# Two blocks on one core: block compression with the weights moving in four column groups, gate activations in table order, the decay moved, operand splits shared

## The chip, the cores and the metric

The program runs on one core of one Trainium2 chip. The metric is the device time of one execution in microseconds (us). The engines are TensorE (PE in the profile, its weight loads PEld), VectorE (DVE), ScalarE (ACT), GpSimd (POOL) and SyncE (SP), which here only issues the loads of weights. TensorE's granted clock has two levels, 2.4 GHz (1.00 in the profile) and 1.2 GHz (0.50).

## The reference

The first block is two layers of attention, pooling, convolution and FFN over 256 tokens and 256 context tokens. The second is one hybrid layer over the 256 tokens of the result, and the change is in it. Cut to what it touches:

```python
# NSA branch: 15 blocks of 32 tokens, stride 16, of k and v, for 2 kv heads
def compress(t, w1, w2):
    tb = t[:, blk_idx] + cmp_pos[None, None, :, None, :]
    tb = tb.transpose(0, 1, 3, 2, 4).reshape(B, n_cmp, G, CMP_BLOCK * dh)   # 2048 features
    return jax.nn.silu(tb @ w1) @ w2                                        # 128 hidden, 64 out
k_c = rms_norm_2(compress(k_cmp, wk1, wk2), kn_g)
v_c = compress(v_cmp, wv1, wv2)
...
# LRU branch
r = jax.nn.sigmoid(...); i_g = jax.nn.sigmoid(...)
log_a = -LRU_C * r * jax.nn.softplus(-lam)
a = jnp.exp(log_a)
b = jnp.sqrt(-jnp.expm1(2.0 * log_a)) * (i_g * xc)
...
# fox branch
c = jnp.cumsum(jax.nn.log_sigmoid(f_logit), axis=1)   # added to the scores
# the branches and their gates
y_a * silu(ga), y_b * silu(gb), y_c * silu(gc), y_d * silu(gd)   # y_d = gelu(ud) * mix(layer_norm(gelu(vd)))
```

## The kernel before

**Products.** Activations lie transposed, 128 features by 256 tokens a tile. Almost every product of weights is made of three matmuls in the type fp32r (`mm3`, lines 354 to 356: hi times hi, hi times lo, lo times hi). `weights()` (lines 339 to 348) brings 128x1024 weights in one 512 KB load issued by SP (line 336), ACT casts them to `whi` (line 344) and DVE subtracts for `wlo` (line 345). The pools hold 4 raw tiles, 3 `whi` and 3 `wlo`, so a cast waits until the products of the third chunk before are done. `split` (lines 350, 351) does the same to an activation. `evac` copies from PSUM in turn on ACT (line 678) and on DVE (line 680).

**Order.** The program is written in the order of its loops, and a list scheduler with a model of the durations sets the order of each engine's instructions from the dependences. `tc.issue_after(i)` adds the edge that what is issued inside comes after `i`.

**Compression** (lines 1137 to 1175). DVE adds the position (line 1137) and gives `tbs[p]`, 128 features by 16 chunks of 32 columns. For k and then for v, 16 fp32 matmuls (line 1146) have a 128x128 chunk of `w1` as the stationary operand and 32 columns of `tbs` as the moving one, and add into 128 hidden by 32 columns; an fp32 matmul is two records in the trace, so there are 64. Silu on ACT (line 1149) gives `hT`. From that of k follow a matmul with `w2` (line 1152), ACT's square (line 1155), DVE and POOL for the norm, DVE `kc` (line 1160) and a transpose (line 1162); from that of v, lines 1166 to 1175.

**Decay and forget gates** (lines 1217 to 1254). `log_sigmoid` is ACT's Abs and Exp and then a series of 20 small DVE operations. It is used for 16 columns of `lsig` (the fox cumulative sum, two matmuls) and for 4 columns of `lam2`, from which `cneg` and `cpos` are scaled.

**NSA heads, gates, fox heads** (lines 1298 to 1580). `jobs` holds 20 projections for branch b and d, and later 8 for `ga` and `gc`; `more(n)` takes n of them between heads. Eight NSA heads (scores, `probs`, `weighted`) run, then `batch` issues the 12 gate activations (Sigmoid, Gelu, Silu) on ACT (line 1458) after the last Exp of the last NSA head. Eight fox heads follow. `probs` puts min and mask on DVE (line 1390), Exp on ACT (line 1393), the scaling on DVE (line 1398). `weighted` has three transposes (line 1421), a copy `aT`, and two matmuls (lines 1424, 1425). After fox head 0, `lru_gates()` issues four times Tanh and Exp in turns (lines 1349, 1350); ACT loads a table whenever a function of another table comes.

**After the fox heads**, `late_gates` and the merge by the mixing gates (lines 1592 and on) follow.

Of the kernel before, what the change touches and what calls it, by code (L numbers as in the profile page):

```python
# [12 lines left out]
F32 = mybir.dt.float32  # L13
# [212 lines left out]
def _constants():  # L226
# [31 lines left out]
    parts["rep"] = rep  # L258
    off, flat = 0, []
# [17 lines left out]
def tile_two_blocks(ctx: ExitStack, tc: tile.TileContext, w: bass.AP, blk: bass.AP, cols: bass.AP,  # L277
# [4 lines left out]
    P = {"nscr": NSCR}  # L282
# [612 lines left out]
    rows = modulation_by_rows()  # L895
    for l in range(DEPTH):
# [91 lines left out]
        for t, (f0, f1) in enumerate(THIRDS):  # L988
# [3 lines left out]
            for f in range(f0, f1):  # L992
# [19 lines left out]
                rows_step(0)  # L1012
            final = t == 2
# [203 lines left out]
    def log_sigmoid(dst, x, n, y_out=None):  # L1217

        e, z, z2, s = (P["wk"].tile([128, 16], F32, name="ls", bufs=5)[:, :n] for _ in range(4))
        act.activation(e, x, AF.Abs)  # L1220
        act.activation(e, e, AF.Exp, scale=-1.0)
        dve.tensor_scalar(z, e, 2.0, None, op0=ALU.add)
        dve.reciprocal(z, z)
        dve.tensor_tensor(z, z, e, op=ALU.mult)
        dve.tensor_tensor(z2, z, z, op=ALU.mult)
        dve.tensor_scalar(s, z2, 2.0 / 17, 2.0 / 15, op0=ALU.mult, op1=ALU.add)
        for i in (13, 11, 9, 7, 5, 3, 1):
            dve.tensor_tensor(s, s, z2, op=ALU.mult)
            dve.tensor_scalar(s, s, 2.0 / i, None, op0=ALU.add)
        dve.tensor_tensor(s, s, z, op=ALU.mult)  # L1230
        dve.scalar_tensor_tensor(dst, x, 0.0, s, op0=ALU.min, op1=ALU.subtract)

    fox_side("ka", "kna", 1.0)
    fox_side("qa", "qna", -0.125)

    ls = P["wk"].tile([128, 2, 8], F32, name="lsig")
    for i, tt in enumerate(TT):
        dve.tensor_tensor(ls[:, i], small[tt][:, 280:288], R("bf"), op=ALU.add)
    log_sigmoid(ls.rearrange("p a b -> p (a b)"), ls.rearrange("p a b -> p (a b)"), 16)
    cneg = P["wk"].tile([128, 4], F32, name="cneg")  # L1240
    cpos = P["wk"].tile([128, 4], F32, name="cpos")
    log_sigmoid(cneg, C("lam2"), 4)
    dve.tensor_scalar(cneg, cneg, 8.0, None, op0=ALU.mult)
    dve.tensor_scalar(cpos, cneg, -1.0, None, op0=ALU.mult)
    for i, tt in enumerate(TT):
        ps = bank("aux")
        for j in range(i + 1):
            pe.matmul(ps[:, :8], K("tri") if j == i else ones, ls[:, j], start=(j == 0), stop=(j == i))
        zq, zk = qk66["qa", tt], qk66["ka", tt]
        dve.tensor_scalar(zq[:, :, 64], ps[:, :8], -1.0, None, op0=ALU.mult)  # L1250
        dve.tensor_copy(zk[:, :, 65], ps[:, :8])
        pool.memset(zq[:, :, 65:66], 1.0)
        pool.memset(zk[:, :, 64:65], 1.0)
# [14 lines left out]
    for i, tt in enumerate(TT):  # L1268
# [24 lines left out]
        evac(pcT[:, i * 128:i * 128 + 128], pt[:, :128])  # L1293

# [88 lines left out]
    last_exp = [None]  # L1383

    def probs(items, gates):
# [3 lines left out]
        for i, (ps, mask, e) in enumerate(items):  # L1389
            dve.tensor_tensor_reduce(e, ps, mask, 1.0, 3.0e38, ALU.add, ALU.min, mn[:, i:i + 1])  # L1390
        with (tc.issue_after(behind[0].ins) if behind[0] else nullcontext()):
            for i, (ps, mask, e) in enumerate(items):
                last_exp[0] = act.activation(e, e, AF.Exp, bias=mn[:, i:i + 1], scale=-1.0, accum_out=sm[:, i:i + 1])  # L1393
# [42 lines left out]
    for hd in range(8):  # L1436
# [23 lines left out]
    batch([(AF.Sigmoid, d[jp], {}) for d in (rg, ig) for jp in range(2)] +  # L1460
          [(AF.Gelu, vd[tt], dict(accum_out=mu[tt])) for tt in TT] +
          [(AF.Gelu, raw["ud", jp], {}) for jp in range(2)] +
          [(AF.Silu, raw[n, jp], {}) for n in ("gd", "gb") for jp in range(2)], last_exp[0])
# [82 lines left out]
    for hd in range(8):  # L1546
# [13 lines left out]
        if hd == 0:  # L1560
            lru_gates()
        elif hd == 2:
# [87 lines left out]
```

## Time and profile before

| what | value |
| --- | --- |
| median of 3 runs | 1428.55 us (1427.30 to 1432.38) |
| the profiled execution, its own time | 1427.89 us |
| its span in the trace | 1426.1 us |
| granted TensorE clock, mean | 0.965 |
| busy: PE, PEld, DVE, ACT, POOL | 1350.7, 1185.2, 965.0, 615.3, 237.4 us |
| HBM read | 210.98 MB, 149 GB/s over the span |

Read it so: PE is busy 95% of the span, but a busy PE may run at half its clock, and its idle time lies in few places. So a stage is judged by three things: PE's busy time there, its idle time with what ended it, and the granted clock.

### The profile page before, as it was taken

What the parts mean: (1) busy time and instruction counts of PE and PEld (TensorE: products, weight loads), DVE (VectorE), ACT (ScalarE), POOL (GpSimd) and SP (SyncE); (2) the same over time, 40 slices, a digit from 0 to 9 for tenths busy, and PEclk for the clock granted to TensorE, in tenths of its full rate; (3) what the DMA queues carried; (4) which work ended last, traced back from release to release, by engine and by line L of the source; (5) the groups of instructions that cost most, each with busy time, mean ns of one, the idle gap of its engine ahead of it and who ended that gap; (6) DMA issues with size and microseconds to landing.
All of it is one profiled execution on the core that took longest, in us unless ns stands there. A gap on an engine that the chain in (4) does not pass through costs nothing. (4 is left out here: it accounts for less than half of the span.)

```text
span 1426.1 us, 22731 instructions
## 1 busy us (share of the span) xinstructions
PE 1350.7 (95%) x8750; PEld 1185.2 (83%) x8750; DVE 965.0 (68%) x1924; ACT 615.3 (43%) x1094; POOL 237.4 (17%) x274
## 2 busy tenths in 40 slices
PE   4999999899999999999988899999989998999999
PEld 2699657788888888888966899999877887988999
DVE  4599666677766677738966655555776666657565
ACT  3334454433222222235355443444634558546443
POOL 0056530410000000014534300000442002000000
PEclk8999999899999999999989899999988999999999
DMA  8423541335445567623301355554733423434553
GB/s 327 181 88 134 172 153 45 134 121 190 160 148 166 192 219 238 209 85 104 119 30 60 119 170 185 171 196 159 243 127 111 141 94 105 134 106 158 181 187 125
DMA packets 61309, 213.52 MB, mean 150 GB/s; under 512 B 6928, under 2 KB 8080, under 8 KB 60944
## 3 DMA queue, kind: packets, MB, share of 16 engines
q1 hardware_dynamic: 60768, 209.90, 43.8%
q10 hardware_dynamic: 432, 2.16, 0.4%
q8 instruction: 69, 1.13, 0.3%
q14 instruction: 40, 0.33, 0.1%
HBM read 210.98 MB, written 1.05 MB: 149 GB/s over the span
## 5 line engine op out<-in xcount | busy, mean ns | idle before, releaser
L344 ACT CAST whi<-wraw 128x1024 fp32r<-128x1024 f32 (+2 forms) x296 | 304.8, 1033 | 534.4 <-PE ps_mm L355 243.4
L345 DVE TENSOR_TENSOR wlo<-wraw,whi 128x1024 fp32r<-128x1024 f32 (+2 forms) x296 | 359.3, 1216 | 173.8 <-ACT whi L344 171.5
L354 PE MATMUL ps_mm<-hH,whi 128*128 128x256 f32 (+1 forms) x1056 | 345.1, 329 | 11.1 <-ACT hH L492 9.0
L355 PE MATMUL ps_mm<-hL,whi 128*128 128x256 f32 (+1 forms) x1056 | 342.3, 325 | 1.7 <-DVE hL L493 1.7
L356 PE MATMUL ps_mm<-hH,wlo 128*128 128x256 f32 (+1 forms) x1056 | 342.0, 325 | 0.9 <-DVE wlo L345 0.8
L354 PEld LDWEIGHTS ps_mm<-hH,whi 128*128 128x128 f32 x1056 | 204.3, 195 | 32.8 <-ACT hH L492 11.1
L355 PEld LDWEIGHTS ps_mm<-hL,whi 128*128 128x128 f32 x1056 | 204.4, 194 | 18.8 <-DVE hL L493 3.1
L356 PEld LDWEIGHTS ps_mm<-hH,wlo 128*128 128x128 f32 x1056 | 204.2, 194 | 17.1 <-DVE wlo L345 2.0
L354 PE MATMUL ps_mm<-hidH,whi 128*128 128x256 f32 (+1 forms) x683 | 214.8, 317 | 3.0 <-ACT hidH L350 1.7
L355 PE MATMUL ps_mm<-hidL,whi 128*128 128x256 f32 (+1 forms) x683 | 215.2, 316 | 0.6 <-DVE hidL L351 0.6
L356 PE MATMUL ps_mm<-hidH,wlo 128*128 128x256 f32 (+1 forms) x683 | 214.4, 316 | 0.0
L355 PE MATMUL ps_mm<-wlo,hH 128*128 128x256 f32 (+2 forms) x464 | 145.5, 315 | 4.1 <-DVE wlo L345 4.0
L356 PE MATMUL ps_mm<-whi,hL 128*128 128x256 f32 (+2 forms) x464 | 143.3, 311 | 0.0
L354 PE MATMUL ps_mm<-whi,hH 128*128 128x256 f32 (+2 forms) x464 | 141.3, 313 | 2.0 <-ACT tm L642 1.5
L354 PEld LDWEIGHTS ps_mm<-hidH,whi 128*128 128x128 f32 x683 | 129.5, 190 | 12.0 <-ACT hidH L350 1.9
L355 PEld LDWEIGHTS ps_mm<-hidL,whi 128*128 128x128 f32 x683 | 129.6, 190 | 9.5 <-DVE hidL L351 1.2
L356 PEld LDWEIGHTS ps_mm<-hidH,wlo 128*128 128x128 f32 x683 | 129.5, 190 | 8.1
L465 POOL TENSOR_TENSOR squares<-squares,scr 128x256 f32<-128x256 f32 (+1 forms) x28 | 31.6, 1127 | 561.5 <-ACT scr L464 561.0
L575 DVE CUSTOM_DVE_ANT_0 ps_md<-wmod,tm 128x512 f32<-128x512 f32 x160 | 111.5, 697 | 10.8 <-DMA wmod<-in_w_dram 7.9
L359 POOL TENSOR_TENSOR st<-st,mhalf 128x4 f32<-128x4 f32 (+3 forms) x54 | 69.1, 1284 | 201.7 <-DVE st L627 88.6
L843 DVE SCALAR_TENSOR_TENSOR xT<-ps_mm,modv,xT 128x256 f32<-128x256 f32 x116 | 52.5, 479 | 73.4 <-PE ps_mm L356 73.4
L355 PEld LDWEIGHTS ps_mm<-wlo,hH 128*128 128x128 f32 x464 | 89.5, 193 | 11.4 <-DVE wlo L345 7.1
(345 smaller groups left out, 2011.6 us busy)
## 6 DMA issues: line engine op xcount, KB each, us to landing
wraw<-in_w_dram SPq DMA_DIRECT2D x271, 512.0 KB, 3.4
wmod<-in_w_dram SPq DMA_DIRECT2D x85, 512.0 KB, 4.2
wraw<-in_w_dram SPq DMA_DIRECT2D x32, 448.0 KB, 3.2
xT<-in_x_dram ACTq DMA_DIRECT2D x2, 1024.0 KB, 6.9
single<-in_w_dram SPq DMA_DIRECT2D x8, 256.0 KB, 7.6
wraw<-in_w_dram SPq DMA_DIRECT2D x4, 288.0 KB, 3.5
tm<-in_rows_dram SPq DMA_DIRECT2D x4, 256.0 KB, 6.5
out_dram<-scr SPq DMA_DIRECT2D x8, 128.0 KB, 1.7
```

What stands on the lines that cost most here:

```text
L344: act.copy(out=hi[:, :m], in_=t[:, :m])
L345: P["split"] = dve.tensor_tensor(lo[:, :m], t[:, :m], hi[:, :m].bitcast(F32), op=ALU.subtract)
L354: pe.matmul(ps, a[0], b[0], start=start, stop=False)
L355: pe.matmul(ps, a[0], b[1], start=False, stop=False)
L356: P["product"] = pe.matmul(ps, a[1], b[0], start=False, stop=stop)
L359: pool.tensor_tensor(t, t, mhalf[:, :n], op=ALU.pow)
L465: eng.tensor_tensor(squares[:, lo:hi], squares[:, lo:hi], q, op=ALU.add)
L575: dve.tensor_tensor_reduce(bank("md"), t[:, i * 512:i * 512 + 512], crow[2 * j + i], 1.0, 0.0, ALU.mult, ALU.add, sums[j][:, i * KD + d:i ...
L843: dve.scalar_tensor_tensor(xT[:, d, r], ps[:, s * 256 - lo:s * 256 - lo + 256], M(l, which, 1 - s)[:, d:d + 1], xT[:, d, r], op0=ALU.mult, ...
```

## The change

- `compress`: the operands change places. The 32 columns of `tbs` are stationary and the 128 columns of `w1` move; the four chunks j of a group q go to four column groups of the array (`tile_position`), so that four partial sums of 32 rows stand on the 128 partitions. k and v share a bank; ACT copies it (`cp`), and two matmuls with a new constant `sum4` (four identities of 32, 32 more columns in one load of constants) add the four partial sums and turn them.
- `decay()`, that is the `log_sigmoid` of `lam2` with `cneg` and `cpos`, is called from the last layer of the first block; the block for `lsig` stands later in the second block.
- The batch of gates comes after all the Exps of the last NSA head, each activation after the one before, `gb` before `gd`. `lru_gates` follows at once, with four Tanh and then four Exp in the same chain, instead of after fox head 0.
- From NSA head 6 to fox head 2 every second weight cast (counted from the start) is made by DVE.

```diff
     def weights(key):
...
-        act.copy(out=hi[:, :m], in_=t[:, :m])
+        P["count"] += 1
+        if P["both"] and P["count"] % 2:
+            dve.tensor_copy(hi[:, :m], t[:, :m])
+        else:
+            act.copy(out=hi[:, :m], in_=t[:, :m])
         P["split"] = dve.tensor_tensor(lo[:, :m], t[:, :m], hi[:, :m].bitcast(F32), op=ALU.subtract)
...
                 rows_step(0)
+                if last and f == 10:
+                    decay()
...
-    for p in "kv":
-        ph = bank("aux")
+    ph = bank("aux")
+    for i, p in enumerate("kv"):
         for q in range(4):
-            t = w1[p, q]
             for j in range(4):
-                jj = q * 4 + j
-                pe.matmul(ph[:, :32], t[:, j * 128:j * 128 + 128], tbs[p][:, jj * 32:jj * 32 + 32],
-                          start=(jj == 0), stop=(jj == 15))
+                o = (q * 4 + j) * 32
+                pe.matmul(ph[j * 32:j * 32 + 32, i * 128:i * 128 + 128], tbs[p][:, o:o + 32],
+                          w1[p, q][:, j * 128:j * 128 + 128], start=(q == 0), stop=(q == 3), tile_position=(0, j * 32))
+    cp = scr()
+    act.copy(out=cp[:, :256], in_=ph[:, :256])
+    for i, p in enumerate("kv"):
+        pe.matmul(ph[:, 256 + i * 32:288 + i * 32], cp[:, i * 128:i * 128 + 128], K("sum4"), start=True, stop=True)
         hT = P["wk"].tile([128, 32], F32, name="hT", bufs=2)
-        act.activation(hT, ph[:, :32], AF.Silu)
+        act.activation(hT, ph[:, 256 + i * 32:288 + i * 32], AF.Silu)
...
     def lru_gates():
         for jp in range(2):
             pool.tensor_tensor(ig[jp], ig[jp], xc[jp], op=ALU.mult)
-            for a in range(2):
-                j = jp * 2 + a
-                c = slice(a * 256, a * 256 + 256)
-                act.activation(xc[jp][:, c], rg[jp][:, c], AF.Tanh, scale=cpos[:, j:j + 1])
-                act.activation(rg[jp][:, c], rg[jp][:, c], AF.Exp, scale=cneg[:, j:j + 1])
+        cols = [(jp, a * 256, jp * 2 + a) for jp in range(2) for a in range(2)]
+        batch([(AF.Tanh, xc[jp][:, o:o + 256], rg[jp][:, o:o + 256], dict(scale=cpos[:, j:j + 1]))
+               for jp, o, j in cols] +
+              [(AF.Exp, rg[jp][:, o:o + 256], rg[jp][:, o:o + 256], dict(scale=cneg[:, j:j + 1]))
+               for jp, o, j in cols], ())
...
+        P["both"] = hd >= 6
         more(2)
...
     def batch(items, then):
-        with tc.issue_after(then.ins):
-            for f, t, kw in items:
-                behind[0] = act.activation(t, t, f, **kw)
...
+        with ExitStack() as order:
+            for i in then:
+                order.enter_context(tc.issue_after(i.ins))
+            for f, out, t, kw in items:
+                with tc.issue_after(behind[0].ins) if behind[0] else nullcontext():
+                    behind[0] = act.activation(out, t, f, **kw)
...
+          same(AF.Silu, [raw[n, jp] for n in ("gb", "gd") for jp in range(2)]), last_exp)
+    lru_gates()
...
-        if hd == 0:
-            lru_gates()
-        elif hd == 2:
+        if hd == 2:
+            P["both"] = False
             lru_mix()
```

In the order of the instructions three places show it (line numbers of the changed kernel are higher: 354 to 356 are 359 to 361, 1458 is 1477, 1393 is 1408, 1421 to 1425 are 1436 to 1440).

PE behind the compression. Line 1182 is the new matmul with `sum4` (in `cstt`) for k, then v, 1187 that with `w2`, 1197 the transpose of `kc`:

```order
L1182 MATMUL ps_aux<-cstt,scr 128x32
L360 MATMUL ps_mm<-wlo,hH 128x512
...
L1182 MATMUL ps_aux<-cstt,scr 128x32
L1187 MATMUL ps_aux<-colt,hT 32x64
...
L1197 MATMUL ps_aux<-first,kc 128x32
L1201 MATMUL ps_aux<-colt,hT 32x64
L1205 MATMUL ps_aux<-st_10441,cstt 128x64
L1217 MATMUL ps_aux<-first,tm 128x128 x8
```

Six weight products stand between the two matmuls with `sum4`, and five between 1187 and 1197; before, 21 stood between the matmul with `w2` and the transpose of `kc` (lines 1152 and 1162).

ACT at the gates, in the changed kernel, from the last Exps of NSA head 7 to the first fox head:

```order
L1477 ACT_TABLE_LOAD
...
L1477 ACT_TABLE_LOAD
L1477 ACTIVATE tm,st_11925<-tm 128x512
...
L1477 ACT_TABLE_LOAD
L1477 ACTIVATE single<-single 128x512
...
L1477 ACTIVATE tm<-tm,cpos 128x256 x4
L1477 ACT_TABLE_LOAD
L1477 ACTIVATE tm<-tm,cneg 128x256
...
L1408 ACTIVATE e,st_11981<-e,st_11980 128x128
```

Four table loads stand there where ten stood (7 of line 1458, 2 of line 1393, 1 of line 1350), and the first Exp of the fox heads needs none. In the whole program ACT has 21 instead of 27.

PE at fox heads 2 to 5. Of line 1546 are the transposes of the fox queries and keys (line 1523 before), on `ps_sc` the scores, and on `ps_mm` with `hH` or `hidH` the weight products. In the changed kernel:

```order
L1440 MATMUL ps_aux<-aT,tm 64x128
L1546 MATMUL ps_aux<-first,z_10568 66x128
...
L361 MATMUL ps_mm<-hH,wlo 128x256
L359 MATMUL ps_sc<-hidH 128x128 x2
...
L361 MATMUL ps_sc<-hidH,hidL 128x256
L1439 MATMUL ps_aux<-aT,tm 64x256
L1440 MATMUL ps_aux<-aT,tm 64x128
L1436 MATMUL ps_aux<-first,e 128x128 x3
L1439 MATMUL ps_aux<-aT,tm 64x256
```

From the values of fox head 2 to those of head 5 there are two weight products among the heads' own work; before, 33 stood between the scores of heads 4 and 5 and those of heads 6 and 7, where now one stands. They now come earlier, between the heads before. On ACT, two weight casts for them stand in a row ahead of the cast of `hidH` that the scores of heads 4 and 5 need.

At the start of the program, DVE has ten operations of `decay` ahead of the first modulation vector `modv` (line 528 before), and others one by one behind it.

## Rows read from the trace of the kernel before

**Rows 1.** The page's first part: busy time of each engine (share of the span) xinstructions.
```profile
PE 1350.7 (95%) x8750; PEld 1185.2 (83%) x8750; DVE 965.0 (68%) x1924; ACT 615.3 (43%) x1094; POOL 237.4 (17%) x274
```
**Rows 2.** Table by stage: window, length, busy us of PE PEld DVE ACT POOL, granted clock, DMA.
```profile
1026.00:1052.80 26.80, 23.59 (x100) 17.50 (x98) 25.86 (x68) 16.59 (x27) 19.77 (x21) 1.00 0.46 158
...
1056.80:1066.20 9.40, 9.40 (x47) 9.16 (x46) 3.91 (x5) 0.40 (x2) 2.37 (x1) 0.50 0.51 167
...
1173.60:1193.40 19.80, 16.09 (x120) 14.30 (x119) 9.35 (x26) 19.59 (x32) 5.00 (x4) 1.00 0.20 67
1193.40:1200.00 6.60, 5.68 (x27) 4.99 (x28) 6.60 (x9) 6.55 (x12) 1.88 (x2) 0.50 0.46 159
```
**Rows 3.** Timeline of PE at the compression: start, us, line, xcount [idle before].
```profile
1054.37 11.54 PE L1146 MATMUL ps_aux<-tm,single 128*128 128x32 f32 x64 [1.54 <-issue]
1065.84 0.42 PE L1152 MATMUL ps_aux<-colt,hT 128*32 128x64 f32 x2
1066.79 0.63 PE L356 MATMUL ps_mm<-whi,hL 128*128 128x512 f32 x1
...
1070.20 0.56 PE L356 MATMUL ps_mm<-whi,hL 128*128 128x512 f32 x1
1070.60 0.39 PE L355 MATMUL ps_mm<-wlo,hH 128*128 128x512 f32 x1
...
1072.87 0.39 PE L356 MATMUL ps_mm<-whi,hL 128*128 128x512 f32 x1
```
**Rows 4.** Waits of PE, 1000 to 1100 us: total, times, longest.
```profile
PE ps_mm L355 <- DVE wlo L345: 4.0, 6, 1.0
PE ps_aux L1146 <- issue: 1.5, 1, 1.5
```
**Rows 5.** Groups of DVE, 1020 to 1054 us: xcount, busy us, mean ns, idle before.
```profile
L1243 DVE TENSOR_SCALAR cneg<-cneg 128x4 f32<-128x4 f32 x1 | 1.6, 1618 | 0.0
...
L1229 DVE TENSOR_SCALAR ls<-ls 128x4 f32<-128x4 f32 x7 | 1.3, 187 | 0.1
```
**Rows 6.** Timeline of PE, fp32 matmuls: plain, then in two column groups (cut at 1226.3, and whole).
```profile
1075.52 1.09 PE L1182 MATMUL ps_aux<-first,tm 128*128 128x128 f32 x8
...
1077.61 0.60 PE L1192 MATMUL ps_aux<-first,tm 128*128 128x128 f32 x4
...
1226.07 0.45 PE L1512 MATMUL ps_mm<-wraw,tm 128*64 128x128 f32 x4
1226.07 0.87 PE L1512 MATMUL ps_mm<-wraw,tm 128*64 128x128 f32 x10
```
**Rows 7.** Timeline of ACT and DVE behind the compression.
```profile
1065.95 0.20 ACT L1149 ACTIVATE hT<-ps_aux 128x32 f32<-128x32 f32 x1 [6.63 <-PE ps_aux L1146]
1067.44 0.46 DVE L1160 SCALAR_TENSOR_TENSOR kc<-ps_aux,st,rowt 32x64 f32<-32x64 f32 x2 [0.65 <-POOL st L1157]
```
**Rows 8.** Groups of ACT at the gates, 1173.5 to 1214 us (columns as in 5).
```profile
L1458 ACT ACT_TABLE_LOAD x7 | 9.0, 1283 | 0.1
```
**Rows 9.** Waits of PE, 1100 to 1240 us.
```profile
PE ps_mm L354 <- ACT whi L344: 2.0, 1, 2.0
PE ps_aux L1424 <- ACT aT L678: 1.7, 1, 1.7
PE ps_aux L1421 <- DVE e L1398: 0.9, 1, 0.9
```
**Rows 10.** Timelines of ACT and PE at fox heads 4 to 7, in order of time.
```profile
1251.50 1.04 ACT L344 CAST whi<-wraw 128x1024 fp32r<-128x1024 f32 x1 [2.30 <-issue]
...
1254.99 0.44 PE L354 MATMUL ps_sc<-hidH 66*128 66x128 f32 x2 [0.72 <-ACT hidH L350]
...
1259.07 0.50 ACT L1393 ACTIVATE e<-e,st 128x256 f32<-128x256 f32 x1
```
**Rows 11.** Timeline of DVE at the start.
```profile
45.75 0.23 DVE L528 TENSOR_TENSOR modv<-ps_sc,colt 128x8 f32<-128x8 f32 x2
46.21 3.26 DVE L490 SCALAR_TENSOR_TENSOR tm<-xT,scale,scr 128x256 f32<-128x256 f32 x8
```

More of the change, by code (lines that the diff above doesn't have):

```diff
@@ L258, in _constants @@
     parts["rep"] = rep
+    parts["sum4"] = np.tile(np.eye(32), (4, 1))
     off, flat = 0, []
@@ L280, in tile_two_blocks @@
     dma, act, dve, pool, pe = nc.sync, nc.scalar, nc.vector, nc.gpsimd, nc.tensor
-    P = {"nscr": NSCR}
+    P = {"nscr": NSCR, "both": False, "count": 0}
     const = ctx.enter_context(tc.tile_pool(name="const", bufs=1))
@@ L895, in tile_two_blocks, with log_sigmoid, decay @@
     rows = modulation_by_rows()
+    def log_sigmoid(dst, x, n, y_out=None):
+        e, z, z2, s = (P["wk"].tile([128, 16], F32, name="ls", bufs=5)[:, :n] for _ in range(4))
+        act.activation(e, x, AF.Abs)
+        act.activation(e, e, AF.Exp, scale=-1.0)
+        dve.tensor_scalar(z, e, 2.0, None, op0=ALU.add)
+        dve.reciprocal(z, z)
+        dve.tensor_tensor(z, z, e, op=ALU.mult)
+        dve.tensor_tensor(z2, z, z, op=ALU.mult)
+        dve.tensor_scalar(s, z2, 2.0 / 17, 2.0 / 15, op0=ALU.mult, op1=ALU.add)
+        for i in (13, 11, 9, 7, 5, 3, 1):
+            dve.tensor_tensor(s, s, z2, op=ALU.mult)
+            dve.tensor_scalar(s, s, 2.0 / i, None, op0=ALU.add)
+        dve.tensor_tensor(s, s, z, op=ALU.mult)
+        dve.scalar_tensor_tensor(dst, x, 0.0, s, op0=ALU.min, op1=ALU.subtract)
+    cneg = const.tile([128, 4], F32, name="cneg")
+    cpos = const.tile([128, 4], F32, name="cpos")
+    def decay():
+        log_sigmoid(cneg, C("lam2"), 4)
+        dve.tensor_scalar(cneg, cneg, 8.0, None, op0=ALU.mult)
+        dve.tensor_scalar(cpos, cneg, -1.0, None, op0=ALU.mult)
     for l in range(DEPTH):
@@ L1215, in fox_side @@
         toks(name, f)
[L1217 to L1231, printed above, removed]
     fox_side("ka", "kna", 1.0)
     fox_side("qa", "qna", -0.125)
[L1236 to L1253, printed above, removed]
     for k in range(KD):
@@ L1293, in tile_two_blocks @@
         evac(pcT[:, i * 128:i * 128 + 128], pt[:, :128])
+    ls = P["wk"].tile([128, 2, 8], F32, name="lsig")
+    for i, tt in enumerate(TT):
+        dve.tensor_tensor(ls[:, i], small[tt][:, 280:288], R("bf"), op=ALU.add)
+    log_sigmoid(ls.rearrange("p a b -> p (a b)"), ls.rearrange("p a b -> p (a b)"), 16)
+    for i, tt in enumerate(TT):
+        ps = bank("aux")
+        for j in range(i + 1):
+            pe.matmul(ps[:, :8], K("tri") if j == i else ones, ls[:, j], start=(j == 0), stop=(j == i))
+        zq, zk = qk66["qa", tt], qk66["ka", tt]
+        dve.tensor_scalar(zq[:, :, 64], ps[:, :8], -1.0, None, op0=ALU.mult)
+        dve.tensor_copy(zk[:, :, 65], ps[:, :8])
+        pool.memset(zq[:, :, 65:66], 1.0)
+        pool.memset(zk[:, :, 64:65], 1.0)
     raw, jobs, count = {}, [], {}
@@ L1382, in tile_two_blocks @@
     behind = [None]
-    last_exp = [None]
+    last_exp = []
     def probs(items, gates):
@@ L1390, in probs @@
             dve.tensor_tensor_reduce(e, ps, mask, 1.0, 3.0e38, ALU.add, ALU.min, mn[:, i:i + 1])
+        last_exp.clear()
         with (tc.issue_after(behind[0].ins) if behind[0] else nullcontext()):
             for i, (ps, mask, e) in enumerate(items):
-                last_exp[0] = act.activation(e, e, AF.Exp, bias=mn[:, i:i + 1], scale=-1.0, accum_out=sm[:, i:i + 1])
+                last_exp.append(act.activation(e, e, AF.Exp, bias=mn[:, i:i + 1], scale=-1.0, accum_out=sm[:, i:i + 1]))
         dve.reciprocal(sm[:, :m], sm[:, :m])
@@ L1455, in batch, with same @@
     def batch(items, then):
-        with tc.issue_after(then.ins):
-            for f, t, kw in items:
-                behind[0] = act.activation(t, t, f, **kw)
[L1460 to L1463, printed above, removed]
+        with ExitStack() as order:
[4 more added lines that the diff above has]
+                    behind[0] = act.activation(out, t, f, **kw)
+    def same(f, ts, **kw):
+        return [(f, t, t, kw) for t in ts]
+    batch(same(AF.Sigmoid, [d[jp] for d in (rg, ig) for jp in range(2)]) +
+          [(AF.Gelu, vd[tt], vd[tt], dict(accum_out=mu[tt])) for tt in TT] +
+          same(AF.Gelu, [raw["ud", jp] for jp in range(2)]) +
+          same(AF.Silu, [raw[n, jp] for n in ("gb", "gd") for jp in range(2)]), last_exp)
+    lru_gates()
     for n in ("ga", "gc"):
@@ L1571, in late_gates @@
         gv = {n: xT[:, o:o + 4, 0:256] for n, o in (("ga", 0), ("gc", 4))}
-        batch([(AF.Sqrt, xc[jp], {}) for jp in range(2)] + [(AF.Silu, gv[n], {}) for n in ("gc", "ga")], last_sig[0])
+        batch(same(AF.Sqrt, [xc[jp] for jp in range(2)]) + same(AF.Silu, [gv[n] for n in ("gc", "ga")]), last_sig)
         lru_scan()
@@ L1587, in tile_two_blocks @@
     last_sig = [None]
-    behind[0] = last_exp[0]
+    behind[0] = last_exp[-1]
     def sig(s, p):
```

## The prediction

> **What bounds the kernel now.** The page's first part comes first: PE is busy for 1350.7 of 1426.1 us, DVE for 965.0, ACT for 615.3 [rows 1]. So the program goes at PE's pace, and what the change is worth is what it takes from PE: work, idle time, or time at half clock. Next comes the table by stage [rows 2]. The reader is to see three stages in it. From 1026 to 1052.8 us DVE is busy 25.86 of 26.8 us, PE 23.59: DVE is the bound there. From 1056.8 to 1066.2 PE is full, but at clock 0.50. From 1173.6 to 1193.4 ACT is busy 19.59 of 19.8 us and PE 16.09: ACT is the bound, and behind it, to 1200, PE runs at 0.50. The timeline then gives the compression, the waits of PE tell on whom it waited [rows 4, 9], and the groups by line what ACT and DVE did meanwhile [rows 5, 8].
>
> The sum is made against the profiled execution, 1427.9 us; the median of the runs shown, 1428.55, lies 0.65 above it, which is added at the end.
>
> **The compression on PE: -6.6 us.** Its 64 records last from 1054.37 to 1065.84, 11.47 us [rows 3]. The new ones have 128 moving columns for 32, and there are 64 again, 16 rounds of four column groups. No row shows four groups. The nearest shows fp32 records of 128 columns in two groups: ten take 0.87 us and the first four of them 0.45, so one more costs (0.87 - 0.45) / 6 = 0.070 us. The same in one group: eight take 1.09 and four 0.60, 0.122 each [rows 6]. I take 64 x 0.070 = 4.5 us, for two groups are the nearest, plus 0.4 for the two matmuls with `sum4` (four records of 32 columns; at half clock one of that width costs 11.47 / 64 = 0.18, so 0.7 at most). 11.47 - 4.9 = 6.6. The ends: no overlap, 64 x 0.122 = 7.8 us, a gain of 3.3; all four overlapping, 16 x 0.122 = 2.0, a gain of 9.1. The Trainium skill (TensorE: Matmul & The Clock Gate, Part 3: Packing small matmuls) says that a weight load overlaps a running matmul only if its row group differs; here all groups share the rows, so by it the gain lies near the small end. The two-group rows speak against that; the case has its own rival below.
>
> **The clock behind it: -2.0 us.** PE ran the compression at 0.50 although it was busy throughout: from 1056.8 on the clock is 0.50, after products at full clock [rows 2]. Behind it the 512-column products go on at half: nine starts from 1066.79 to 1070.20, 0.426 apart, then eleven from 1070.60 to 1072.87, 0.227 apart [rows 3]; with the one before them ten products lose 0.2 us each. If 128 columns keep PE at full clock, these 2.0 us go; at worst none.
>
> **DVE ahead of it: -2.5 us.** The decay's small operations leave this stage: 14 of some 0.185 us are 2.6, the scaling of `cneg` 1.6 [rows 5], and nine single ones of 0.15 to 0.35. PE waited there 4.0 us for `wlo` (about 0.8 of it behind the compression) and 1.5 at the compression, where nothing shows as the releaser but the position adds on DVE had just ended [rows 4]. So 4.7 us at most, and I take a little over half, because the 16-column series only moves later and DVE stays near full; 0.5 at least.
>
> **The new waits of the chain: +1.4 us.** Between PE's last partial sum and `kc` stand the copy `cp`, the sum, Silu, the square and the norm. From Silu to the end of `kc` it took 1065.95 to 1067.90, 2.0 us [rows 7], covered by 21 products. In the new order sixteen stand beside `cp` and six beside Silu, which cover them, and five beside the norm: 5 x 0.227 = 1.1 us for 2.0, so 0.9 is open, and behind that the v part follows back to back, two steps of ACT or DVE that I put at 0.5 together. Ends: 0 and 2.5.
>
> **The gates: -6.7 us.** Six table loads fewer at 1.283 us [rows 8] are 7.7 us of ACT, where ACT is the bound. PE's idle time there is 2.0 + 1.7 + 0.9 = 4.6 us [rows 9], and at half clock it worked 5.68 us [rows 2], which at the ratio 0.227 / 0.426 would be 2.65 shorter. PE cannot gain more than the 7.25 of both; ACT's 7.7 covers that, so PE is the bound next. I take 6.7, since a copy `aT` still waits on ACT's line at the last NSA heads; at least 2.5, if only one wait goes. The four casts on DVE lie in a stage where DVE is busy 9.35 of 19.8 us and cost nothing; without this room each is about a microsecond in front of its own `wlo`.
>
> **The fox heads: +5.2 us.** Here the order speaks against the change. The weight products of this stage are the same, but come earlier, and between the values of heads 2 and 5 PE has two left. Two casts stand on ACT ahead of the cast of `hidH` that the scores of heads 4 and 5 need; one such cast waited 2.30 us for its buffer already before [rows 10]. From the first score product of a pair (1254.99) to its last Exp (1259.57) pass 4.6 us [rows 10], of which PE fills about 2.7 with that pair's scores, transposes and values: 1.9 open. With 0.9 and 0.7 at the next two heads (half of that chain, for one head each) this is 2.3 + 1.9 + 0.9 + 0.7 = 5.8, where 1.4 stood (0.72 in [rows 10], and about as much at heads 6 and 7): +4.4. A stretch with so much idle time may cost the clock as behind the gates; a third of the 2.65 there is 0.8. Ends: 0, if the earlier end of the gates lets the chains run ahead, and 7.5, with the whole 2.65.
>
> **The start: +1.2 us.** Ten operations of the decay come ahead of `modv`, which now starts at 45.75, followed by the eight operations on which the first `hH` waits [rows 11]. They depend on one another and on ACT's Abs and Exp, which need a table load moved up. At 0.185 they are 1.9 us, part of it in idle time of DVE, and three more stand one by one between the following ones. Ends 0.3 and 2.0. The load of constants is 16 KB larger; it is not waited for, 0.
>
> Sum: -6.6 - 2.0 - 2.5 + 1.4 - 6.7 + 5.2 + 1.2 = -10.0, so 1417.9 for the profiled execution and **1418.5** for the median.
>
> **The rivals.**
> - *Everything overlaps.* Four groups run together (gain 9.1 for 6.6) and the fox heads lose nothing (0 for 5.2): 1418.5 - 2.5 - 5.2 = 1410.8. For it: two groups nearly halve the record already. Against it: the order at heads 3 to 5. The Trainium skill's span of a packed round, in the same section (one matmul's duration and some nanoseconds a tile), leads here; no run shows it for fp32.
> - *The gates' gain is given back.* PE arrives earlier at the fox heads, and has the same idle time there: gates at -2.5 and fox heads at +7.5, 1418.5 + 4.2 + 2.3 = 1425.0. For it: the products that covered the heads are used up earlier.
> - *The groups don't overlap*, so the change does not do there what it is written for: 64 x 0.122 us, 1418.5 + 3.3 = 1421.8. For it: a weight load precedes each record. Against: [rows 6].
> - *The gate chain becomes a wall* (slower). Each gate activation now waits for the one before, and all Exps of the fox heads for the last. Before, the chain of 26.1 us of ACT work (19.59 + 6.55, [rows 2]) left holes that others used. If some gate projection comes late, everything behind stands: all eight heads then run without weight products. Five heads more at 1.9 are 9.5 us, and the half clock over some 20 us of PE work there about 9: 1437. It decides from the point at which the last gate Exp ends about 7 us behind PE's last weight product ahead of head 0; by 7.7 us less of loads it should end before it.
>
> **How the numbers follow.** Forecast 0.50 (its own range 1413 to 1422), everything overlaps 0.15, given back 0.18, no overlap 0.10, wall 0.07. The range 1410 to 1426 holds the first four but for their tails and leaves out the wall. No change within 0.5% (what a measurement of this kernel can tell) reaches 7.1 us down, to 1421.4, and up to 1435.7. Faster: 0.45 of the forecast, all of the first rival, and under half of the third, with a little of the second: 0.66. Slower is nearly all of the wall: 0.06. The rest, 0.28, is within.
>
> **What would show it.** Right: the 64 records of the new compression in some 4.5 us and at clock 1.00, with products 0.227 apart behind it; fewer than 2 us of waits for `wlo` from 1026 on; four table loads at the gates and PE's idle time there under 1 us; an idle time of 4 to 6 us at fox heads 2 to 5; `modv` a microsecond later. Wrong: records of 0.12 us in the compression; ACT still without a gap at the gates while PE waits; waits at every fox head; or a difference in the first block, where only the order of some operations moved, of more than 2 us.

## The result, and the profile after

| kernel | median us (runs) | before, same call | ratio to before, 95% interval |
| --- | --- | --- | --- |
| the changed kernel | 1411.51 (4) | 1430.01 | 0.9877 (0.9842 to 0.9913) |
| the same, repeated | 1415.79 (11) | 1427.12 | 0.9918 (0.9886 to 0.9949) |

It is faster by some 0.8 to 1.2%. The forecast of 1418.5 us lay above both medians, the range held them. Single runs scatter widely (1410.2 to 1426.2 us in the repeat, 1419.8 to 1437.8 before), so stages are compared rather than totals. Ratios leave out a run more than 1.5% above the fastest of its kernel; there is one, of the gates alone, at 1444.97 us. The profiled execution took 1412.22 us (span 1410.4), against 1427.89.

Weight products are the same in all kernels: each trace has 7323 records of them. So a stretch runs here from the start of one product, counted from the first, to the start of another: to the 5150th (first block and what precedes the compression; below it is called the first block), the 5600th (compression), the 6300th (gates and fox heads), and the last (merge). In us, with the PE time lost to half clock in brackets where there was any (PE busy times one minus the granted clock, over windows of 2 us):

| kernel | to 5150 | to 5600 | to 6300 | to the end |
| --- | --- | --- | --- | --- |
| before | 1024.7 (26.1) | 143.3 (10.2) | 127.3 (3.0) | 127.5 (1.6) |
| changed, first profile | 1031.1 (33.7) | 127.3 | 123.1 | 125.4 (1.5) |
| changed, repeated | 1034.6 (38.0) | 127.7 | 127.3 (7.2) | 125.2 (1.4) |
| compression alone | 1030.8 (35.1) | 131.0 (1.7) | 128.3 (4.4) | 126.6 (3.1) |
| gates alone | 1027.1 (30.3) | 143.2 (10.2) | 129.4 (8.7) | 128.6 (3.1) |
| constants wider, unused | 1022.8 (26.7) | 141.6 (8.6) | 126.4 (2.7) | 125.4 (1.6) |
| decay back | 1036.5 (39.0) | 130.0 | 127.8 (7.3) | 125.4 (1.6) |
| earlier gate end | 1029.4 (28.3) | 127.4 | 120.2 (1.5) | 126.6 (3.0) |
| the same, repeated | 1028.2 (32.9) | 127.4 | 118.7 | 126.1 (2.7) |

So the compression stretch gained 16 us, the first block lost 6 and more, gates and fox heads gained 4 in one profile and nothing in the other, and the merge gained 2 that nobody had forecast. What the first block lost is half clock: without it the block takes 998.6 us before, 997.4 and 996.7 after.

The page's first part after the change, to set beside [rows 1]:

```profile
PE 1340.1 (95%) x8754; PEld 1172.3 (83%) x8754; DVE 964.5 (68%) x1928; ACT 602.9 (43%) x1085; POOL 233.0 (17%) x274
```

The timeline of PE at the compression answers to [rows 3]:

```profile
1057.98 1.96 PE L1177 MATMUL ps_aux<-single,tm 128*32 128x128 f32 x64 [0.49 <-issue]
...
1060.46 0.40 PE L361 MATMUL ps_mm<-whi,hL 128*128 128x512 f32 x1
...
1061.84 0.39 PE L359 MATMUL ps_mm<-whi,hH 128*128 128x512 f32 x1
...
1067.71 0.24 PE L1197 MATMUL ps_aux<-first,kc 32*128 32x32 f32 x1 [0.33 <-DVE kc L1195]
...
1068.47 0.43 PE L1205 MATMUL ps_aux<-st,cstt 32*128 32x64 f32 x2 [0.29 <-ACT st L683]
```

The 64 records took 1.96 us where 11.47 stood, 0.031 each. The products behind are 0.23 apart at once (six steps from 1060.46 to 1061.84). The new waits of the chain are 0.33 and 0.29 us.

The table by stage, columns as in [rows 2], shows the gates and the fox heads:

```profile
1057.90:1060.10 2.20, 1.96 (x64) 1.72 (x64) 2.19 (x5) 0.11 (x1) 0.00 (x0) 1.00 0.00 0
...
1158.50:1180.00 21.50, 21.50 (x151) 18.33 (x150) 16.66 (x43) 14.69 (x34) 5.62 (x4) 1.00 0.27 87
1180.00:1200.00 20.00, 20.00 (x170) 20.00 (x170) 12.36 (x19) 14.51 (x27) 4.03 (x4) 1.00 0.50 160
...
1229.60:1248.30 18.70, 12.97 (x88) 10.03 (x87) 12.06 (x40) 10.67 (x28) 0.00 (x0) 1.00 0.17 57
```

PE is now full at the gates, at 1.00, and ACT has room (14.69 of 21.50 us); four table loads stand there:

```profile
L1477 ACT ACT_TABLE_LOAD x4 | 5.1, 1283 | 0.1
```

At fox heads 2 to 7, from 1229.6 to 1248.3 us, PE is idle for 5.73 of 18.7 us. Four of the seven waits, in the order of their size (total, times, longest):

```profile
PE ps_aux L1436 <- DVE e L1413: 1.0, 1, 1.0
PE ps_aux L1436 <- DVE hidL L356: 1.0, 1, 1.0
PE ps_mm L359 <- ACT e L1614: 0.9, 1, 0.9
PE ps_sc L360 <- DVE hidL L356: 0.9, 1, 0.9
```

Two of the seven, 1.6 us, are weight products on `ps_mm`; `e` of line 1614, for which one of them waits, is the Sigmoid of the merge (line 1592 before). The other five, 4.2 us, are the chain of each pair: cast of `hidH`, the subtraction for `hidL`, scores, mask, Exp, scaling, transposes. Before, from 1240 to 1262 us, PE waited 3.3 us there, 2.0 at the same two products and 1.4 in the chain:

```profile
PE ps_mm L354 <- ACT e L1592: 1.3, 1, 1.3
PE ps_sc L354 <- ACT hidH L350: 0.7, 1, 0.7
PE ps_aux L1424 <- DVE aT L680: 0.6, 1, 0.6
PE ps_mm L355 <- DVE hidL L351: 0.6, 1, 0.6
```

So the chain's idle time grew by 2.8 us, and all of it by 2.4.

### The profile page after: what moved, and what is told of

Same layout as the page of the kernel before. It is cut to its first block, busy times and chain, and to the rows that moved or that the text cites. A ratio compares the mean times of both kernels' runs of the same rounds, so it can differ in the third digit from the quotient of the medians.

```text
span 1410.4 us, 22740 instructions
## 1 busy us (share of the span) xinstructions
PE 1340.1 (95%) x8754; PEld 1172.3 (83%) x8754; DVE 964.5 (68%) x1928; ACT 602.9 (43%) x1085; POOL 233.0 (17%) x274
## 5 line engine op out<-in xcount | busy, mean ns | idle before, releaser
L349 ACT CAST whi<-wraw 128x1024 fp32r<-128x1024 f32 (+2 forms) x292 | 300.5, 1033 | 528.4 <-PE ps_mm L360 271.5
L359 PEld LDWEIGHTS ps_mm<-hH,whi 128*128 128x128 f32 x1056 | 204.2, 195 | 32.9 <-ACT hH L497 9.3
L364 POOL TENSOR_TENSOR st<-st,mhalf 128x4 f32<-128x4 f32 (+3 forms) x54 | 64.4, 1198 | 200.1 <-DVE st L632 88.1
```

What stands on the lines that cost most here:

```text
L359: pe.matmul(ps, a[0], b[0], start=start, stop=False)
L364: pool.tensor_tensor(t, t, mhalf[:, :n], op=ALU.pow)
```

## The experiments

**The compression alone.** The kernel before with this edit:

```diff
+                pe.matmul(ph[j * 32:j * 32 + 32, i * 128:i * 128 + 128], tbs[p][:, o:o + 32],
+                          w1[p, q][:, j * 128:j * 128 + 128], start=(q == 0), stop=(q == 3), tile_position=(0, j * 32))
...
+    act.copy(out=cp[:, :256], in_=ph[:, :256])
+    for i, p in enumerate("kv"):
+        pe.matmul(ph[:, 256 + i * 32:288 + i * 32], cp[:, i * 128:i * 128 + 128], K("sum4"), start=True, stop=True)
```

> The kernel before with the new compression alone (weights moving in four column groups, the copy, the matmuls with sum4); decay, gates and casts as before. Theory (the compression is worth about 15 us of its stage, through 9.5 us of shorter records, the 2 us of half clock behind it and some 3.4 us of a second stretch at half clock from 1084 to 1091 us that goes with it): 1414 to 1418 us, 64 records in 2.0 us, granted clock 1.00 from 1026 to 1110 us. Rival (much of the stage's gain belongs to the decay's DVE operations that left it, or the second stretch at half clock has its own cause): 1420 to 1424 us, with that stretch still there. The first block of this kernel is that of before: if its stretch from 165 to 300 us takes as long as before within 1 us in this trace, the 3 us more of the changed kernel there belong to the change; if it scatters by several us, they are chance.

Measured: 1415.75 us (8 runs), ratio 0.9917 (0.9884 to 0.9951), so about all that the repeat of the whole change gained. The table by stage:

```profile
1054.00:1062.00 8.00, 5.74 (x80) 4.20 (x78) 7.91 (x14) 2.15 (x3) 1.12 (x1) 1.00 0.19 67
1062.00:1100.00 38.00, 37.30 (x179) 28.72 (x180) 27.62 (x54) 20.81 (x33) 10.98 (x12) 0.96 0.45 153
```

The clock, 0.50 in [rows 2], is 1.00 and 0.96. The stretch took 131.0 us for 143.3: 12 of the 16 us are the compression's, 9.5 of them in its records (11.47 us before, 1.95 here). What half clock cost in the whole stretch, inside those records and behind them, fell from 10.2 us to 1.7 (one piece at 0.50 from 1080.9 us, where the theory had 1.00 throughout); the second piece of it, from 1084 to 1091 us before, is among what went. The first block has the order of before and yet took 6 us longer: 133.6 us for 126.2 between the 700th and the 1050th product (165 to 300 us). So the 3 us more of the changed kernel there need no cause in the change.

**The gates alone.** The batch behind all last Exps, `gb` before `gd`, the four Tanh and four Exp in its chain; compression, decay and casts as before.

```diff
-        if hd == 0:
-            lru_gates()
-        elif hd == 2:
+        if hd == 2:
...
+          same(AF.Silu, [raw[n, jp] for n in ("gb", "gd") for jp in range(2)]), last_exp)
+    lru_gates()
```

> The kernel before with the gates alone (batch in table order, each activation behind the one before, lru_gates in the same chain; no cast on DVE, decay and compression as before). Theory (gates -6.4, fox heads +2.4): 1424 to 1427 us; PE idle under 1.5 us from the first gate to fox head 1 and about 5.7 us at fox heads 2 to 7; four table loads. Rival (the gain in this stage comes from the casts on DVE): within 1 us of before, with 3 us or more of waits for whi or aT left at the gates.

Measured: 1431.48 us (10 runs), ratio 1.0015 (0.9977 to 1.0053): no change. The waits at the gates went (0.4 us left), but neither theory has what came instead, in the table by stage:

```profile
1242.00:1248.00 6.00, 4.47 (x29) 3.52 (x30) 3.21 (x10) 3.05 (x7) 0.00 (x0) 0.96 0.49 175
1248.00:1254.00 6.00, 4.35 (x16) 2.45 (x15) 2.64 (x12) 1.41 (x7) 0.00 (x0) 0.50 0.00 0
1254.00:1260.00 6.00, 5.46 (x23) 4.42 (x22) 3.29 (x12) 2.70 (x6) 0.00 (x0) 0.50 0.01 3
```

PE waits at the fox heads, and its clock falls to 0.50 there for some 20 us, in which it loses 8.7 us. This is the second rival of the prediction in kind, not in its sizes: the gates kept their gain, the idle time grew less at the heads, and the clock took 8.7 us, where the rival had 2.65. The whole stretch took 129.4 us for 127.3.

**The decay back in the second block.**

```diff
-                if last and f == 10:
-                    decay()
...
     log_sigmoid(ls.rearrange("p a b -> p (a b)"), ls.rearrange("p a b -> p (a b)"), 16)
+    decay()
```

> The changed kernel with the decay's operations called in the second block behind the forget gates, all else as changed. Theory (the decay at the start costs its 1.2 us there, and the further 5 us of the first block, 3.0 at 165 to 300 us and 2.6 at 640 to 860 us, are chance): 1.2 us less up to 75 us in the trace, other stretches of the first block scattered; in the second block 1 to 2 us of waits for wlo come back; 1410 to 1413 us. Rival A (the whole 6.6 us of the first block come from the moved decay): 1404 to 1407 us. Rival B (DVE was what bounded the stage ahead of the compression, and gets the decay back): 1414 to 1416 us.

Measured: 1413.84 us (10 runs), ratio 0.9909 (0.9876 to 0.9942), no different from the changed kernel. The compression stretch is 130.0 us, 2.3 to 2.6 above the changed kernel: this is the price of the decay on DVE there. The first block took 1036.5 us, no less than with the decay ahead, and 39.0 of them went to half clock, although its order of instructions is that of before. So the total does not tell the two places apart.

**The groups' matmuls one after another.**

```diff
-        for q in range(4):
-            for j in range(4):
+        for j in range(4):
+            for q in range(4):
```

> The changed kernel with the two inner loops of the compression exchanged: the four matmuls of one column group follow one another (8 records), then those of the next group. The output is the same. Theory (records of different column groups overlap only where they are neighbours in the order): the 64 records take 6 to 7.5 us, about 0.1 each, and the total is 4 to 6 us above the changed kernel, 1415 to 1418 us. Rival (the groups overlap whatever the order): 2.0 to 2.5 us, and the time of the changed kernel.

Measured: one run, 1421.84 us, where the scatter of single runs leaves the total open. In the timeline the records took neither 6 to 7.5 nor 2.0 to 2.5 us:

```profile
1061.33 4.30 PE L1177 MATMUL ps_aux<-single,tm 128*32 128x128 f32 x64 [0.49 <-issue]
```

That is 4.30 / 64 = 0.067 each, close to the 0.070 of the two-group rows in [rows 6]. So the order of the matmuls sets how far groups overlap: 0.031 a record when the group changes with every matmul, 0.067 when it changes after four. Both theories fall; overlap is neither for direct neighbours alone nor free of the order. The starts of the records show it more finely: in the middle eight records start within 0.467 us, 0.058 each; the first four and the last four, which have no other group beside them, start 0.109 apart.

**One column group.** All 16 chunks add up in the same 32 partitions (the copy and the matmuls with `sum4` take 32 partitions too):

```diff
-                pe.matmul(ph[j * 32:j * 32 + 32, i * 128:i * 128 + 128], tbs[p][:, o:o + 32],
-                          w1[p, q][:, j * 128:j * 128 + 128], start=(q == 0), stop=(q == 3), tile_position=(0, j * 32))
+                pe.matmul(ph[0:32, i * 128:i * 128 + 128], tbs[p][:, o:o + 32],
+                          w1[p, q][:, j * 128:j * 128 + 128], start=(q + j == 0), stop=(q + j == 6), tile_position=(0, 0))
```

> The changed kernel with the compression in one column group: each 32 columns of tbs stationary, 128 columns of w1 moving, all 16 chunks added up in the same 32 partitions, no column groups beside one another. Theory (what the groups give is the overlap, 0.109 us a record alone): the 64 records take 7.0 us at full clock. For the clock, theory A (it fell before because the records had only 32 moving columns): 1.00 throughout and behind it. Theory B (it falls with work that fills little of the array, whatever moves): 0.50 in a part of the 7 us or behind it, and the records near 0.12 to 0.2.

Measured: one run, 1424.38 us. Timeline, and table by stage:

```profile
1053.22 7.15 PE L1177 MATMUL ps_aux<-single,tm 128*32 128x128 f32 x64 [0.51 <-issue]
...
1069.53 0.24 PE L1197 MATMUL ps_aux<-first,kc 32*128 32x32 f32 x1 [1.69 <-DVE kc L1195]
```
```profile
1053.70:1060.50 6.80, 6.80 (x63) 6.60 (x61) 5.86 (x8) 0.09 (x1) 2.54 (x1) 1.00 0.58 180
1068.00:1076.00 8.00, 6.18 (x23) 5.20 (x24) 4.21 (x11) 3.83 (x10) 2.89 (x3) 0.60 0.01 2
```

7.15 us, 0.11 a record, at 1.00 throughout. With 32 moving columns the clock had fallen by 1056.8, 2.4 us after the start [rows 2, 3]; with 128 it held for 7 us although only 32 columns of the array were used. So the first half of theory A came, 1.00 throughout, but not its second: the clock fell to 0.50 at 1069.6 us, behind the idle 1.69 us at `kc`, and this run can't tell whether the compression had a part in that. Nor were the kernels alike ahead of the records: PE was idle for 2.5 of the 10 us before them in the kernel before and for 0.5 here. Why the clock fell before stays open.

**Wider constants.** The kernel before with `parts["sum4"] = np.tile(np.eye(32), (4, 1))` among the constants and nothing that reads it.

> The kernel before with the 32 columns of sum4 added to the constants and never read, nothing else. Theory (the merge after the fox heads is 2 us shorter in every kernel with the new compression because the wider constants move the addresses of the tiles behind them): the time from the 6300th weight product to the last, without idle time and half clock, falls from 122.3 to 120 us, and the stage before it from 23.65 to 23.43, although no instruction of the merge differs. Rival (it comes with the new order or with the bank that the compression frees): 122.3 stays.

Measured: one run, 1421.36 us. The merge takes 125.4 us for 127.5, 120.2 without idle time and half clock, as the theory said. Timeline of PE for the same 24 weight products, first and last, of the kernel before:

```profile
1320.04 0.28 PE L354 MATMUL ps_mm<-hidH,whi 128*128 128x256 f32 x1
...
1322.76 0.28 PE L356 MATMUL ps_mm<-hidH,wlo 128*128 128x256 f32 x1
```

and with the wider constants:

```profile
1315.43 0.29 PE L355 MATMUL ps_mm<-hidH,whi 128*128 128x256 f32 x1
...
1318.05 0.28 PE L357 MATMUL ps_mm<-hidH,wlo 128*128 128x256 f32 x1
```

23 steps take 2.72 us and 2.62: 0.118 and 0.114 a product. The merge has 480 of these, 1.9 us. In all profiles the merge takes 119.9 to 120.3 us without idle time and half clock where the constants are wider, and 122.0 or 122.3 in the two where they are not. Names, shapes and order of PE's instructions in the merge are the same in this kernel as in the one before; what differs is a tile that is 128 bytes a partition wider, and with it the place of tiles laid out behind it. That the addresses set the pace is inferred from this; no run changed them alone, or tried why these are better.

**An earlier end of the gates.** From here on the changed kernel is altered to give back what the fox heads lose. First, the four Tanh go ahead of the Silu of `gd`, and the four Exp of the LRU behind the Exps of fox heads 0 and 1:

```diff
-          same(AF.Silu, [raw[n, jp] for n in ("gb", "gd") for jp in range(2)]), last_exp)
-    lru_gates()
+          same(AF.Silu, [raw["gb", jp] for jp in range(2)]), last_exp)
+    for jp in range(2):
+        pool.tensor_tensor(ig[jp], ig[jp], xc[jp], op=ALU.mult)
+    batch(lru_tanh() + same(AF.Silu, [raw["gd", jp] for jp in range(2)]), ())
...
+        if hd == 0:
+            lru_exp()
```

> The changed kernel with the four Tanh of lru_gates ahead of the Silu of gd and its four Exp behind the Exps of fox heads 0 and 1, so that the gate chain ends 3.5 us earlier. Theory (the fox heads run out of weight products because 80 of them are used up waiting for the gate chain, and the half clock there comes from the idle time): about 30 products more are left for heads 2 to 5, PE idle time at the fox heads 3 us or less instead of 5.7, no stretch at 0.50 behind it, 3 to 8 us below the runs of the changed kernel that fell to half clock, so 1405 to 1411 us. Rival (PE is the bound up to head 0 anyway, and the idle time at the heads comes from the order of ACT's casts): idle time within 1 us of the changed kernel's, time within 2 us.

Measured: 1410.94 us (4 runs), ratio 0.9872 (0.9838 to 0.9906); gates and fox heads 120.2 us. The waits of PE there add up to 3.3 us, the same four as before. Between the scores of heads 4 and 5 and those of heads 6 and 7 PE has some 30 weight products again, where the changed kernel had hardly any. The theory stands but for 0.3 us of idle time and a short dip of the clock (1.5 us lost).

**Products held for each head.** In addition the job behind head h may start its products only behind the scores of head h+1:

```diff
+        with tc.issue_after(P["hold"].ins) if start and P["hold"] else nullcontext():
+            pe.matmul(ps, a[0], b[0], start=start, stop=False)
...
+        held = P["product"] if 1 <= hd < 7 else None
...
+        P["hold"] = held
         more(1)
+        P["hold"] = None
```

> As early9, and the weight products of the job behind fox head h (h from 1) may start only after the last score product of head h+1, so that each head has one job beside it. Theory (with products beside each head its chain is covered): PE idle under 2 us from head 2 to head 7 and no half clock there; 1404 to 1410 us. Rival (the products held back are missing ahead of head 0, where PE then waits for the gate chain): 3 us or more of idle time at heads 0 and 1, and no better than the changed kernel.

Measured: 1412.47 us (4 runs), ratio 0.9870 (0.9842 to 0.9899). The waits of PE from the gates to the merge:

```profile
PE ps_aux L1439 <- DVE e L1416: 2.8, 1, 2.8
PE ps_aux L1442 <- DVE aT L686: 0.9, 1, 0.9
```

Both are at head 0, as the rival said, and heads 2 to 7 wait for 1.3 us in all, as the theory said. The median lies above the theory's 1404 to 1410 us: it is no gain over the version without.

**Held one head less.** The same with the scores of head h itself as the limit.

> As early1, but the products of the job behind head h wait for the last score product of head h itself, not of the next, so that two jobs may run ahead of head 0's transposes. Theory (early1 lacked some 31 products' time, 3.7 us, ahead of head 0, and this gives 24 back and leaves one job beside each pair): idle time under 1.5 us from the gates to the merge, no stretch at 0.50 there, 1404 to 1409 us, 2 to 6 us below the changed kernel of the same call. Rival (the Exps of head 0 still end later than the products last, and the clock falls for it): 2 us or more of idle time at head 0, and the time of early1.

Measured: 1415.68 us (12 runs), ratio 0.9908 (0.9876 to 0.9940). Waits:

```profile
PE ps_sc L360 <- ACT hidH L355: 1.5, 2, 0.8
PE ps_sc L361 <- DVE hidL L356: 1.5, 1, 1.5
PE ps_aux L1442 <- DVE aT L686: 1.1, 1, 1.1
```

The theory fails, in idle time and in the total. No wait for the Exps of a head is left, but 4.1 us for `hidH`, `hidL` and `aT`: products held back don't cover what stands ahead of the scores. The stretch took 123.1 us. The total shows no difference to the repeat of the changed kernel in the same call; the profiled execution spent 1041.6 us in the first block, more than any other, and shows how that block's scatter covers 4 us here.

**The changed kernel repeated.**

> The changed kernel once more, unaltered, beside the next two on one chip. Theory (the one profile of it missed a stretch at half clock at fox heads 2 to 7 by chance, since three other kernels with the same idle time there lost 7 to 9 us to it): this profile shows 5 us or more at 0.50 between the gates and the merge, and the median lies at 1410 to 1415 us. Rival (its idle time there is split so that the clock holds): no such stretch again, as in the first profile.

Measured: 1415.79 us (11 runs). The fox heads, in the table by stage:

```profile
1236.00:1242.00 6.00, 4.48 (x19) 3.32 (x19) 3.61 (x14) 2.34 (x9) 0.00 (x0) 0.65 0.25 87
1242.00:1248.00 6.00, 4.44 (x16) 2.67 (x17) 2.42 (x8) 1.26 (x3) 0.00 (x0) 0.50 0.00 0
1248.00:1254.00 6.00, 6.00 (x25) 5.05 (x26) 3.75 (x13) 2.86 (x10) 0.00 (x0) 0.50 0.01 3
```

The theory stands, but for a median 0.8 us above its range. Of seven profiles with the new gate order and no remedy, six lost 5.6 to 8.7 us here to half clock; the first of the changed kernel was the exception. The idle time alone does not decide it: from the gates to the merge it was 4.7 to 5.9 us in the six and 7.0 in the exception.

**All casts on ACT.** Without `P["both"] = hd >= 6`.

> The changed kernel with all weight casts on ACT. Theory (the four casts on DVE take 4 us from ACT's chain at the gates, but PE is the bound there by now): idle time at the gates 0 to 1.5 us more, the total within 2 us of the changed kernel. Rival (ACT is still the bound at the gates and needs the room): 3 to 4 us more idle time there, and as much in the total.

Measured: 1412.28 us (7 runs), ratio 0.9900 (0.9866 to 0.9935); at the gates PE waits 0.6 us, with the casts on DVE 1.3 in the first profile and 0.2 in the repeat. The median lies 3.5 us below that of the repeat in the same call, and the intervals overlap: sharing the casts gains nothing here.

**The earlier end of the gates, repeated.**

> The kernel of early9 once more, with more rounds (four runs before gave 1410.94 us and 0.9872). Theory (its gain of some 7 us over the changed kernel at the gates and fox heads, 120.2 against 127.2 us from the first gate to the merge, is real): that stretch again within 2 us of 120.2, and a median of 1406 to 1411 us, 0.984 to 0.989 of before. Rival (that one profile was spared as the first one of the changed kernel was): the stretch near 127 us with a long piece at 0.50, and a median near 1415.

Measured: **1405.57 us** (5 runs, 1403.4 to 1410.7), ratio 0.9857 (0.9833 to 0.9882). Of the versions run it has the lowest median. Its interval ends at 0.9882, just below that of the repeat of the change (from 0.9886, in another call), and overlaps that of the change's first four runs (0.9842 to 0.9913), so the total alone does not settle the gain. The stretch does: it took 118.7 us, with no half clock, as the theory said; the table by stage, 25 us around the fox heads:

```profile
1225.00:1250.00 25.00, 21.66 (x165) 19.16 (x164) 15.01 (x42) 13.78 (x32) 0.00 (x0) 1.00 0.29 100
```

## Why the prediction was right, and where its sizes were off

The direction and the bottleneck held: PE sets the pace, and the gain is work, idle time and half clock taken from it. The order of the gains did not: the gates, the largest term, gave nothing by themselves, and the compression alone gave about as much as the repeat of the whole change. The first four runs lie 0.7 us from the first rival (1410.8), the repeat between it and the forecast; of that rival's two conditions the full overlap came, and fox heads that lose nothing did not. By its own steps:

- **Compression on PE (-6.6 forecast, -9.1 the far end).** The records measured 11.47 to 1.96 us, a gain of 9.5 before the matmuls with `sum4`. The step that failed is the choice of the price 0.070 "for two groups are the nearest". That row was no law of two groups but of its order: line 1512 changes the group after every second matmul. Nor was 0.070 the price of its overlap: the paired records of the row start 0.055 apart, and the last two of the ten have no neighbour. The exchanged loops gave 0.067 with four groups. The full overlap of the far end is what happened. The Trainium skill (TensorE: Matmul & The Clock Gate, Part 3: Packing small matmuls) says that weight loads overlap running matmuls only where the row groups differ. Here all share them, and 64 records and their weight loads (PEld, 1.72 us busy) took 1.96 us together, so the trace disagrees.
- **The clock (-2.0).** Right in kind, too small. Before lost 10.2 us to half clock in this stretch, in three places: in the records themselves, in the ten products behind, and from 1084 to 1091 us, where the forecast had not looked (none of its rows covers it). With the compression alone 1.7 us were left.
- **DVE (-2.5).** 2.3 to 2.6 by the decay put back: right.
- **The chain (+1.4).** 0.33 + 0.29 of waits: within the ends, less than taken.
- **Gates (-6.7) and fox heads (+5.2).** The gates' part was right: idle time from 4.6 to 1.3 us, no half clock. For the fox heads the forecast had 5.8 us of idle time in the pairs' chains where 1.4 stood, +4.4. The 5.73 of the first profile look like it, but 1.6 of them are the two weight products, which waited 2.0 before: the chains stood at 4.2, +2.8. And "a third of the 2.65" for the clock, 0.8 us, was mis-sized: 5.6 to 8.7 us in six of seven profiles. (The far end of 7.5 us is 0.45 more than its terms, 4.4 and 2.65, make.) So in the repeat the two terms add up to nothing, and the gates alone measured 1.0015. The rival "the gates' gain is given back" is what happened in this stage in those six, by the clock more than by idle time. The remedy shows the cause: with the chain of gates ended earlier, products were left for the heads, and the stretch took 7 to 9 us less than in the profiles of the changed kernel and its variants that fell to half clock (127.2 to 127.8 us), 3 to 4 less than in the one that was spared.
- **Start (+1.2).** Not settled. Up to the 100th product it took 66.4 us before, 67.6 and 68.2 after, but 64.1 to 66.4 in kernels that left it alone and 64.9 to 67.8 in the others with the decay ahead. `modv` started at 45.40 and 46.08 us for 45.75, so the microsecond forecast there did not come.
- **What the forecast did not have.** The merge gained 2.1 us, by addresses as far as is known. The first block lost 6 to 10 us, and that is half clock: 26.1 us of it before, 33.7 and 38.0 after. Five kernels with the order of before there (before, the compression alone, the gates alone, the wider constants, the decay back) lost 26.1 to 39.0 us, and took 1022.8 to 1036.5; without half clock all fourteen profiles took 995 to 1001. So no cost of the moved decay is shown, and the runs don't tell whether it makes half clock likelier. In the second layer the nine profiles with the decay ahead, in which some operations changed places, took 219.5 us and more, up to 227.4; the four without the decay ahead or any of its parts took 216.5 to 216.9, but the kernel with the decay back, whose order there is that of before, took 219.2.
- **Its own signs.** Four table loads, clock 1.00 at the compression and 0.23 a product behind it came. Waits for `wlo` from 1026 us on were 2.1 and 2.4 us, not under 2, and PE's idle time at the gates 1.3 and then 0.2. One sign of being wrong came: the first block differs by more than 2 us.

The sum, for the first profile: -10.0 was forecast; 6.3 more went at the compression, 2.6 more at gates and fox heads and 2.1 in the merge, and 5.2 more came in the first block: -15.8, with -15.7 measured (1407.0 for 1422.7 us up to the last product). In the repeat the first block came to 8.7 more and gates and fox heads to 1.5 more, -8.0 in all. So the forecast lies between the two executions because errors of opposite sign, none of them small, stand against each other: that the total came out so near is luck.

## What to carry to other kernels

A small matmul that shares the array with others overlaps as far as its order lets it: alternate the column groups with every matmul, and take no price from a row with another order. Shortening the chain that holds up one stage spends the work that covers the next; end the chain earlier where functions share a table, so that products are left for the heads behind it. Price idle time in a stage of small matmuls with the clock that goes with it, here 5.6 to 8.7 us beside 4.7 to 5.9 of idle time.

## What was not expected of the hardware

- With 128 bytes a partition of unused constants, 480 matmuls elsewhere came 0.004 us closer each, 2.1 us in all with smaller effects on the others.
- Half clock cost the first block 26.1 to 39.0 us in the five kernels whose first block has the order of before. A single profile of a stage in which the clock falls says little: the same fox heads lost 0 in one execution and 7.2 us in another.
- The clock held 1.00 through 7.15 us of matmuls with 128 moving columns in one column group, and fell to 0.50 within 2.4 us of matmuls with 32 moving columns on the full array, which had more idle time ahead of them.
